# Two-layer trunk on one core: all FFN column blocks by seven products instead of two plain blocks at each start

## The chip, the cores and the metric

The kernel runs on one core of one Trainium2 chip. The metric is the device time of one execution in microseconds (us). TensorE (PE) multiplies matrices; VectorE (DVE) and ScalarE (ACT) work element by element and read PE's results out of PSUM; GpSimd (POOL) does little here; SyncE (SP) issues the loads of weights. Each engine works through its own queue in a fixed order and stands still where an instruction waits for another engine or a transfer.

## The reference

640 tokens (128 context and 512 latent) of width 1024 pass two layers. Each layer is an FFN with half a step, a token mixer, and a second FFN; so there are four FFNs, and they hold most of the work:

```python
def swiglu(h, w_in, w_out):
    u, v = jnp.split(h @ w_in, 2, axis=-1)
    return (jax.nn.silu(u) * v) @ w_out

def ffn_branch(x, mods, g_pre, g_post, w_in, w_out):
    shift, scale, gate = mods
    y = swiglu(modulate(x, g_pre, shift, scale), w_in, w_out)
    return x + FFN_RES * gate * rmsnorm(y, g_post)
```

`w_in` is 1024 x 5632 (u and v of 2816 columns each), `w_out` 2816 x 1024. The mixer of the first layer is a gated delta rule beside a latent attention, that of the second a gated linear attention. All of it is float32.

## The kernel before

**Precision.** A float32 operand is split into a high part (a cast to the fast format, on ACT) and a low part (the difference, on DVE). One product of operands is then high x high, high x low and low x high. `pair` does this for weights (L603 and L604, 128x1024 or 128x512), `parts` for tokens (L513 and L514), `close` for the finished block (L691).

**Blocks and products.** The 22 column blocks t of an FFN take 128 columns of u and 128 of v. Tokens are halved (320 each) and so are the features (four chunks of 128 each), so h is a 2x2 of quarters "11", "21", "12", "22". What this document calls a product is one quarter, or a sum of quarters, times one weight half: 4 chunks x 3 split terms = 12 matmuls of 320 columns (`dot`, L650). Directly, u and v of a block need eight products (96 matmuls). In the other form, `rest` with `begin` and `begun`, seven products (84 matmuls) do it, in the manner of Strassen: 1 and 2 use the quarters "11" and "21" as they are, 6, 5, 7 and 4 use sums of quarters (`t2`, `t1`, `t3`, `t4`), 3 uses "22" after the sums. The sums of tokens are formed once in an FFN (`sums`: four differences, L519, then their splits), the sums of weights in each block (`weights_b`, L620 to L623, then three `pair`s for products 6 and 3, 5, and 7 and 4).

**Order of an FFN before.** Two blocks (`PLAIN`) go by eight products: `plain(t, 0)` for t = 0 and 1 uses the first token half, `plain(t, 1)` the second. Between them blocks 2 to 4 are begun by products 1 and 2 (`early`), which need no sums. Then come `open_c`, the sums, the raw loads and `weights_b` of block 2, and the main loop from t = 2 to 21 with `rest`. From block 5 on, product 1 of the next block is put into `rest` of the one before. From t = 2, too, the `down` products of the two blocks closed before (L298, 512 columns, groups of six matmuls) are put between the products of `rest`, at the places that `SLOTS` names; DVE adds each group to y (L304). While the tokens of the first half come in, the kernel also runs mixer or norm rows; the token quarters are split as they arrive.

**Reading results.** DVE reads the accumulator Y after product 6 (L707: u2), again after product 7 (L715: d1, L717 adds Z) and after product 4 (L724, L725); Z, with products 5 and 3, is read in L717, L742 and L744.

**Buffers.** `rawp` is a ring of seven raw weight buffers of 512 KB, `hlp` has 16 split weight buffers, `Tp` 18 token-wide tiles, `ps_up` three accumulators. A program sets the order within each queue when the kernel is built.

## Time and profile before

| | |
|---|---|
| median of three runs | 2714.4 us (2713.94 to 2716.94) |
| the profiled execution | 2716.26 us |
| its span | 2714.5 us |
| mean granted TensorE clock | 0.991 |
| busy share PE / DVE / ACT / POOL | 97% / 72% / 43% / 5% |
| FFN starts, about | 44, 1015, 1478 and 2269 us |

The span is the time from the first to the last instruction of the profile. Busy times of an engine overlap those of others; matmuls are pipelined, so how long a matmul holds PE is read from the distance between starts and not from the duration of one. The granted clock is the mean TensorE clock in a stretch as a share of full speed. An entry in square brackets behind an instruction is the idle time of its engine just before it and what ended it.

### The profile page before, as it was taken

The numbers are of one execution on the slowest core, as the hardware profiler recorded it, in microseconds if no ns is written. First come the engines' busy times: TensorE is split into PE (matmuls) and PEld (weight loads), VectorE is DVE, ScalarE is ACT, GpSimd is POOL, SyncE is SP. The second block draws the span as 40 slices with busy tenths as digits, with TensorE's granted clock in tenths as the row PEclk, the third lists the DMA queues.
The fourth block names the chain that finished last, engine by engine and source line by source line (L and its number), as shares of the span: only waits on it lengthen the run. The fifth ranks groups of instructions, "written<-read, shape, count | busy, mean of one in ns | idle before, by whom it ended". The sixth has DMA issues, their size and how long they took to land. (4 is left out here: it accounts for less than half of the span.)

```text
span 2714.5 us, 41232 instructions
## 1 busy us (share of the span) xinstructions
PE 2632.5 (97%) x16040; PEld 2331.2 (86%) x16040; DVE 1943.0 (72%) x3731; ACT 1179.1 (43%) x2281; POOL 125.5 (5%) x301
## 2 busy tenths in 40 slices
PE   6999999999999999999999999999999999999998
PEld 4988888789858678888997999999899988999997
DVE  5777777768585558777778777777675749777776
ACT  5433333554345645332335433334765447333333
POOL 0000000200100010000001000000200002000001
PEclk8999999999999999999999999999999999999999
DMA  8334424734151334343227322224212143332222
GB/s 272 123 115 141 148 96 133 251 103 142 50 188 46 128 117 130 114 138 103 86 71 244 104 87 86 86 81 135 92 55 67 59 140 109 95 92 86 78 70 101
DMA packets 297099, 309.60 MB, mean 114 GB/s; under 512 B 13573, under 2 KB 250639, under 8 KB 296903
## 3 DMA queue, kind: packets, MB, share of 16 engines
q1 hardware_dynamic: 278240, 260.05, 30.1%
q10 hardware_dynamic: 18663, 46.92, 4.9%
q8 instruction: 126, 2.06, 0.3%
q14 instruction: 70, 0.57, 0.1%
HBM read 286.59 MB, written 20.33 MB: 113 GB/s over the span
## 5 line engine op out<-in xcount | busy, mean ns | idle before, releaser
L650 PE MATMUL up<-ar,hi 128*128 128x320 f32 x2944 | 658.6, 311 | 10.5 <-ACT ar L513 4.5
L650 PEld LDWEIGHTS up<-ar,hi 128*128 128x128 f32 x2944 | 502.4, 189 | 37.2 <-ACT ar L513 6.1
L650 PE MATMUL up<-ar,lo 128*128 128x320 f32 x1472 | 455.5, 310 | 0.6 <-DVE lo L604 0.6
L603 ACT CAST hi<-raw 128x1024 fp32r<-128x1024 f32 x256 | 268.1, 1050 | 295.4 <-PE up L650 258.4
L304 DVE TENSOR_TENSOR y<-y,dn 128x512 f32<-128x512 f32 x388 | 264.5, 682 | 151.9 <-PE dn L298 150.8
L604 DVE TENSOR_TENSOR lo<-raw,hi 128x1024 fp32r<-128x1024 f32 x256 | 312.4, 1222 | 75.1 <-ACT hi L603 74.5
L298 PE MATMUL dn<-hi,al 128*128 128x512 f32 x880 | 347.8, 395 | 0.1
L298 PE MATMUL dn<-lo,ah 128*128 128x512 f32 x880 | 347.6, 395 | 0.0
L298 PE MATMUL dn<-hi,ah 128*128 128x512 f32 x880 | 346.8, 395 | 0.7 <-DVE y L304 0.5
L650 PE MATMUL up<-hq,hi 128*128 128x320 f32 x1408 | 315.1, 310 | 0.3 <-DVE xn L707 0.3
L650 PEld LDWEIGHTS up<-ar,lo 128*128 128x128 f32 x1472 | 277.9, 189 | 1.3 <-DVE lo L604 1.3
L208 PE MATMUL up<-ar,hi 128*128 128x384 f32 (+1 forms) x1184 | 267.3, 315 | 4.9 <-ACT ar L274 4.0
L650 PEld LDWEIGHTS up<-hq,hi 128*128 128x128 f32 x1408 | 238.8, 188 | 21.5 <-issue 9.2
L650 PE MATMUL up<-hq,lo 128*128 128x320 f32 x704 | 217.4, 309 | 0.0
L208 PEld LDWEIGHTS up<-ar,hi 128*128 128x128 f32 x1184 | 200.6, 191 | 15.3 <-issue 5.6
L183 DVE TENSOR_TENSOR lo<-raw,hi 128x1024 fp32r<-128x1024 f32 x145 | 175.8, 1218 | 45.0 <-ACT hi L182 38.2
L298 PEld LDWEIGHTS dn<-hi,al 128*128 128x128 f32 x880 | 165.3, 188 | 39.3 <-DVE al L691 1.2
L298 PEld LDWEIGHTS dn<-hi,ah 128*128 128x128 f32 x880 | 165.2, 188 | 26.3 <-DVE y L304 1.4
L208 PE MATMUL up<-ar,lo 128*128 128x384 f32 (+1 forms) x592 | 184.3, 311 | 0.0
L298 PEld LDWEIGHTS dn<-lo,ah 128*128 128x128 f32 x880 | 165.1, 188 | 22.2
L182 ACT CAST hi<-raw 128x1024 fp32r<-128x1024 f32 x145 | 150.9, 1048 | 44.5 <-PE up L208 19.0
L658 ACT COPY h<-up 128x320 f32<-128x320 f32 x68 | 29.0, 426 | 314.3 <-PE up L650 314.3
(704 smaller groups left out, 4216.2 us busy)
## 6 DMA issues: line engine op xcount, KB each, us to landing
raw<-in_ffn_w_in_dram SPq DMA_DIRECT2D x188, 512.0 KB
mw<-in_mod_w_dram SPq DMA_DIRECT2D x144, 512.0 KB
raw<-in_ffn_w_out_dram SPq DMA_DIRECT2D x88, 512.0 KB
xdr<-x ACTq DMA_DIRECT2D x25, 512.0 KB
x<-xdr ACTq DMA_DIRECT2D x25, 512.0 KB
raw<-in_od_w_in_dram SPq DMA_DIRECT2D x24, 512.0 KB
raw<-in_ev_w_in_dram SPq DMA_DIRECT2D x19, 512.0 KB
gb<-gate ACTq DMA_DIRECT2D x12, 512.0 KB
```

Of the source, the lines that this page charges most:

```text
L182: nc.scalar.copy(hi, raw)
L183: nc.vector.tensor_sub(lo, raw, hi.bitcast(F32))
L208: self.nc.tensor.matmul(ps[:, :n], lhsT=wt[a][:, kc], rhs=self.h[g][:, b, kc], start=k == 0, stop=k == 3 * KC - 1)
L298: nc.tensor.matmul(ps, lhsT=a(i, m), rhs=w[j][:, nh * 512:nh * 512 + 512], start=k == 0, stop=k == last)
L304: nc.vector.tensor_add(yd, yd, ps)
L603: nc.scalar.copy(hi, raw[:, :n])
L604: nc.vector.tensor_sub(lo, raw[:, :n], hi.bitcast(F32))
L650: nc.tensor.matmul(ps[:, :HT], lhsT=w[i][:, kc], rhs=b[j].at(kc), start=first and n == 0, stop=n == 11, skip_group_check=not first)
L658: self.T.nc.scalar.copy(p1, X[:, :HT])
```

## The change

`PLAIN` and `plain` go. `EARLY` is 7 instead of 5: the first seven blocks begin with products 1 and 2, and the main loop runs from t = 0 instead of 2. Down products still start at t = 2. The quarter "12" is no longer split, and its four tiles go; `Tp` is 20 instead of 18 and `rawp` 6 instead of 7. The prefetch loads u of three blocks where it was u and v of two. For the first seven blocks u is loaded twice, once for products 1 and 2 and once for `weights_b`.

```diff
@@ -27,9 +27,8 @@
 GROUPS = ((0, 384), (384, 256))
 HW = (6400, 4096)
 HT = TOK // 2
-PLAIN = 2
 FILLS = (((16, 6), (10, 6)), ((18, 0), (0, 0)))
-EARLY = 5
+EARLY = 7
 SLOTS = ((2, 3, 4, 5, 6), (0, 1, 2, 3, 4))
 TW = 648
 MFILL = ((1, 1, 1, 1, 1, 1, 0), (1, 1, 1, 1, 1, 1, 0), (1, 0, 1, 0, 1, 0, 0), (0, 0, 0, 0, 0, 0, 0))
@@ -87,9 +86,9 @@
         self.cst = mk("cst", 1)
         self.hp = mk("hp", 1)
         self.xp = mk("xp", 5)
-        self.rawp = mk("rawp", 7)
+        self.rawp = mk("rawp", 6)
         self.hlp = mk("hlp", 16)
-        self.Tp = mk("Tp", 18)
+        self.Tp = mk("Tp", 20)
         self.sml = mk("sml", 2)
         self.ps_up = mk("ps_up", 3, space=PSUM)
         self.ps_dn = mk("ps_dn", 2, space=PSUM)
@@ -490,11 +489,8 @@
         return [Quad((t, 4 * HT * (j + i), 0, 4)) for i in range(2)]
 
     def open_b(self):
-        T = self.T
-        self.a1 = T.arena(1)
-        t = [T.T(F32R, "hq") for _ in range(4)]
+        self.a1 = self.T.arena(1)
         self.B["22"] = self.pair_in(self.a1, 0)
-        self.B["12"] = [Quad((t[2 * j], 0, 0, 2), (t[2 * j + 1], 0, 2, 2)) for j in range(2)]
 
     def open_c(self):
         T = self.T
@@ -554,8 +550,7 @@
         if span:
             if m == 3:
                 self.open_b()
-            for n in ("12", "22"):
-                self.parts(self.F[n], n, *span)
+            self.parts(self.F["22"], "22", *span)
             self.spans.append(span)
 
     def first(self, mods, rows):
@@ -580,7 +575,8 @@
                     for o, e, s in segs:
                         t = xT[half * 4 + j][:, o:e]
                         T.modulate(t, t, s, half * 4 + j, *self.mod, j % 2)
-                    self.parts(self.F[n], n, 0, HT, (j,))
+                    if n in self.B:
+                        self.parts(self.F[n], n, 0, HT, (j,))
         self.spans.append((0, HT))
 
 
@@ -628,12 +624,10 @@
     def weights_d(self, t):
         self.wd[t] = self.T.prep_rows(self.w_out, t * P)
 
-    def prefetch(self, ts=range(PLAIN)):
+    def prefetch(self, ts=range(3)):
         for t in ts:
             if (t, 1) not in self.w:
                 self.weights_a(t)
-            if (t, "v1") not in self.w:
-                self.pair(t, self.load(DFF + t * P), "v1", "v2")
 
 
 
@@ -662,24 +656,6 @@
         self.product(X, t, 2, False, True)
         self.T.nc.scalar.activation(s1, X[:, :HT], AF.Silu)
         self.began[t] = None, p1, s1
-
-    def plain(self, t, g):
-
-        T, nc = self.T, self.T.nc
-        if g == 0:
-            self.began[t] = T.T(name="o")
-        o = self.began[t]
-        oc = o[:, g * HT:(g + 1) * HT]
-        for names, v in (((1, 2), False), (("v1", "v2"), True)):
-            ps = T.up()
-            for j, name in enumerate(names):
-                self.dot(ps, self.w[t, name], f"{j + 1}{g + 1}", j == 0, j == 1)
-            if v:
-                nc.vector.tensor_mul(oc, oc, ps[:, :HT])
-            else:
-                nc.scalar.activation(oc, ps[:, :HT], AF.Silu)
-        if g == 1:
-            self.close(t, self.began.pop(t)[:, :TOK])
 
     def close(self, t, a, c=0):
 
@@ -766,22 +742,16 @@
     def run(self, nxt):
         T, n, e, sts = self.T, NFT, EARLY, {}
         self.todo, self.slots = None, ()
-        for t in range(PLAIN):
-            self.plain(t, 0)
-        for t in range(PLAIN, e):
-            self.weights_a(t)
+        for t in range(e):
+            self.prefetch((t,))
             self.early(t)
-        for t in range(PLAIN):
-            self.plain(t, 1)
         self.open_c()
         for c, w in self.spans:
             self.sums(c, w)
         st = T.S([P, D], "xn", 1)
-        self.raws(PLAIN)
-        self.weights_b(PLAIN)
-        for t in range(PLAIN):
-            self.weights_d(t)
-        for t in range(PLAIN, n):
+        self.raws(0)
+        self.weights_b(0)
+        for t in range(n):
             if t + 1 < n:
                 self.raws(t + 1)
             if e <= t + 1 < n:
@@ -799,7 +769,7 @@
             if t % 2 == 1 and t < n - 4:
                 self.weights_d(t - 1)
                 self.weights_d(t)
-            if self.fills[0] > t - PLAIN:
+            if self.fills[0] > t - 2 >= 0:
                 self.filler()
             if self.later and t == 5:
                 self.later()
```

As counts of the whole program: PE has 14,794 matmuls after 14,890; DVE 3,736 instructions after 3,670 (eight more 1024-wide and eight more 512-wide low halves of weights, eight more of each of L620 to L623 and of the evacuations in `rest`, 16 fewer of L678 and some 40 fewer token splits); SP 525 after 509 (16 more loads of 512 KB).

The order of PE at the second FFN start, before: the last rows of the second plain block (v of the second token half, into `up1318`), and then product 6 of block 2 into `up1346`. `ar` and `hq` are token splits, `hi`, `lo` and `hilo` weight splits.

```order
L650 MATMUL up1318_9867<-ar1284_9531,hi1249_9370 128x320 x2
L650 MATMUL up1318_9867<-ar1284_9531,lo1250_9371 128x320
L650 MATMUL up1346_9990<-hq1321_9897,hi1333_9963 128x320 [waits DVE_49]
L650 MATMUL up1346_9990<-hq1322_9898,hi1333_9963 128x320
L650 MATMUL up1346_9990<-hq1321_9897,lo1334_9964 128x320
```

After: the last rows of block 6's product 2 into `up1316`, then product 6 of block 0 into `up1336` and its product 5 into `up1337`.

```order
L644 MATMUL up1316_9754<-ar1238_9267,hi1313_9749 128x320 x2
L644 MATMUL up1316_9754<-ar1238_9267,lo1314_9750 128x320
L644 MATMUL up1336_9862<-hq1317_9781,hi1329_9847 128x320 [waits Activation_49]
L644 MATMUL up1336_9862<-hq1318_9782,hi1329_9847 128x320 [waits DVE_49]
L644 MATMUL up1337_9876<-hq1319_9783,hilo1331_9851 128x320 [waits Activation_49]
L644 MATMUL up1337_9876<-hq1321_9785,hilo1331_9851 128x320 [waits DVE_49]
L644 MATMUL up1336_9862<-hq1317_9781,lo1330_9848 128x320 [waits DVE_49]
```

The plain products that stood ahead of the first sums product are gone; products of early blocks stand there, 168 matmuls in place of 264. Further on in block 0, PE's order after is product 7, product 4 and product 3 with nothing in between:

```order
L644 MATMUL up1336_9862<-hq1324_9788,lo1333_9855 128x320
L644 MATMUL up1336_9862<-ar1238_9267,hi1332_9854 128x320 [waits DVE_49]
...
L644 MATMUL up1336_9862<-ar1238_9267,lo1333_9855 128x320
L644 MATMUL up1337_9876<-ar1287_9531,hi1329_9847 128x320 [waits DVE_49]
```

The first of these rows is the last of product 7, the second begins product 4, the last begins product 3. In blocks from 2 on, rows of down products (L298 before, L288 after) stand between them.

The order of DVE at the same start, before: behind the last token split, the low halves of block 2's weights, the down weights' splits (L183), an evacuation and the closing of a plain block (L678, L691), and the weight sums of block 3.

```order
L514 TENSOR_TENSOR hq1328_9904<-f1231_9260,hq1328_9904 128x128 [waits Activation_49]
L604 TENSOR_TENSOR lo1334_9964<-raw1330_9954,hi1333_9963 128x1024 [waits PE_49,Activation_49]
L604 TENSOR_TENSOR hilo1335_9967<-s11332_9958,hilo1335_9967 128x512 [waits DMAHW5_49,Activation_49]
L604 TENSOR_TENSOR lo1337_9971<-raw1331_9956,hi1336_9970 128x1024 [waits PE_49,Activation_49]
L183 TENSOR_TENSOR lo1340_9977<-raw1338_9974,hi1339_9976 128x1024 [waits DMAHW2_49,DVE_49,Activation_49]
L678 TENSOR_TENSOR o1292_9577<-o1292_9577,up1314_9811 128x320 [waits PE_49]
L183 TENSOR_TENSOR lo1343_9983<-raw1341_9980,hi1342_9982 128x1024 [waits DMAHW4_49,Activation_49]
L691 TENSOR_TENSOR al1316_9838<-o1292_9577,ah1315_9837 128x640 [waits Activation_49]
L620 TENSOR_TENSOR s11361_10110<-raw1345_9988 128x512 [waits DMAHW7_49]
```

After: behind the last token split, the low halves of block 0's weights, the evacuation of block 0's product 6 (L683), and weight sums and low halves of block 1 (L616 to L619, L600) between the evacuations of block 0.

```order
L510 TENSOR_TENSOR ar1287_9531<-f1236_9265,ar1238_9267 128x128 [waits Activation_49]
L600 TENSOR_TENSOR lo1330_9848<-raw1326_9838,hi1329_9847 128x1024 [waits PE_49]
L600 TENSOR_TENSOR hilo1331_9851<-s11328_9842,hilo1331_9851 128x512 [waits DMAHW0_49,Activation_49]
L600 TENSOR_TENSOR lo1333_9855<-raw1327_9840,hi1332_9854 128x1024 [waits PE_49,Activation_49]
L683 TENSOR_TENSOR xn1325_9837<-up1336_9862,e1291_9561 128x320 [waits PE_49]
L616 TENSOR_TENSOR s11340_9936<-raw1335_9860 128x512 [waits DMAHW1_49,DVE_49]
L617 TENSOR_TENSOR raw1335_9860<-raw1334_9858,raw1335_9860 128x512 [waits DMAHW7_49,DVE_49]
L618 TENSOR_TENSOR raw1334_9858<-s11340_9936,raw1334_9858 128x512 [waits DVE_49]
L600 TENSOR_TENSOR hilo1343_9945<-s11340_9936,hilo1343_9945 128x512 [waits Activation_49]
L619 TENSOR_TENSOR raw1334_9858<-raw1334_9858 128x512 [waits DVE_49]
L691 TENSOR_TENSOR xn1325_9837<-up1336_9862,e1291_9561 128x320 [waits PE_49]
```

The evacuations of `rest` (L683, L691 after) now stand where the plain block's last evacuation and the down weights' splits stood.

## Rows read from the trace of the kernel before

**Rows 1.** The page's first part: busy us, share of the span, instructions, by engine

```profile
PE 2632.5 (97%) x16040; PEld 2331.2 (86%) x16040; DVE 1943.0 (72%) x3731; ACT 1179.1 (43%) x2281; POOL 125.5 (5%) x301
```

**Rows 2.** Windows of three main loops: stretch, us, busy per engine, PEclk, DMA share, GB/s

```profile
88.00:460.00 372.00, 367.85 (x2201) 329.66 (x2200) 266.37 (x404) 123.36 (x169) 0.00 (x0) 1.00 0.39 124
1064.00:1424.00 360.00, 359.94 (x2146) 328.05 (x2145) 267.18 (x400) 124.07 (x173) 0.00 (x0) 1.00 0.33 103
2324.00:2660.00 336.00, 336.00 (x1989) 312.53 (x1988) 251.03 (x377) 117.88 (x163) 0.00 (x0) 1.00 0.25 77
```

**Rows 3.** Windows of the four stretches ahead of the first sums product: PE, PEld, DVE, ACT, POOL

```profile
45.00:82.00 37.00, 35.98 (x221) 34.96 (x221) 36.61 (x76) 30.39 (x63) 0.00 (x0) 0.91 0.35 110
1014.00:1062.00 48.00, 43.47 (x278) 41.43 (x278) 45.09 (x87) 33.11 (x75) 6.36 (x9) 0.96 0.46 141
1484.00:1517.00 33.00, 33.00 (x223) 31.92 (x222) 32.36 (x65) 20.97 (x47) 0.00 (x0) 1.00 0.46 144
2285.00:2314.00 29.00, 29.00 (x196) 28.40 (x195) 28.70 (x61) 18.31 (x42) 0.00 (x0) 1.00 0.32 96
```

**Rows 4.** Timeline of PE in a steady block: start, us, engine, line, operation

```profile
107.19 1.92 PE L650 MATMUL up<-hq,hilo 128*128 128x320 f32 x12
108.95 0.39 PE L298 MATMUL dn<-hi,ah 128*128 128x512 f32 x1
...
111.27 0.40 PE L298 MATMUL dn<-lo,ah 128*128 128x512 f32 x1
```

**Rows 5.** Timeline of DVE ahead of the first sums product, at the four starts

```profile
68.80 4.64 DVE L514 TENSOR_TENSOR hq<-xT,hq 128x320 fp32r<-128x320 f32 x11
...
80.00 2.35 DVE L604 TENSOR_TENSOR lo<-raw,hi 128x1024 fp32r<-128x1024 f32 x2
...
1049.45 3.51 DVE L514 TENSOR_TENSOR hq<-f,hq 128x576 fp32r<-128x576 f32 x9 [0.27 <-ACT hq L513]
...
1053.05 1.23 DVE L604 TENSOR_TENSOR lo<-raw,hi 128x1024 fp32r<-128x1024 f32 x1
1054.20 0.68 DVE L604 TENSOR_TENSOR hilo<-s,hilo 128x512 fp32r<-128x512 f32 x1
1054.84 1.23 DVE L604 TENSOR_TENSOR lo<-raw,hi 128x1024 fp32r<-128x1024 f32 x1
...
1058.65 0.81 DVE L691 TENSOR_TENSOR al<-o,ah 128x640 fp32r<-128x640 f32 x1
1059.38 0.68 DVE L620 TENSOR_TENSOR s<-raw 128x512 f32<-128x512 f32 x1
...
1061.55 0.70 DVE L623 TENSOR_TENSOR raw<-raw 128x512 f32<-128x512 f32 x1
...
1507.97 1.21 DVE L604 TENSOR_TENSOR lo<-raw,hi 128x1024 fp32r<-128x1024 f32 x1
...
2305.11 1.22 DVE L604 TENSOR_TENSOR lo<-raw,hi 128x1024 fp32r<-128x1024 f32 x1 [0.20 <-ACT hi L603]
```

**Rows 6.** Timeline of PE: the first matmuls of the first sums product, four starts

```profile
88.31 0.46 PE L650 MATMUL up<-hq,hi 128*128 128x320 f32 x2
...
1063.13 0.46 PE L650 MATMUL up<-hq,hi 128*128 128x320 f32 x2
...
1519.03 0.46 PE L650 MATMUL up<-hq,hi 128*128 128x320 f32 x2
...
2314.03 0.46 PE L650 MATMUL up<-hq,hi 128*128 128x320 f32 x2
```

**Rows 7.** A wait of PE (timeline), and PE-only windows around it: PE busy, PEclk

```profile
998.47 1.90 PE L257 MATMUL pt<-ident,xn 128*128 128x128 f32 x8 [2.78 <-DVE xn L252]
...
995.00:1000.00 5.00, 2.22 (x12) 0.85 0.26 105
1000.00:1005.00 5.00, 5.00 (x22) 0.81 0.00 0
1005.00:1010.00 5.00, 5.00 (x30) 1.00 0.00 0
```

## The prediction

> **What bounds the kernel now.** I read the busy shares first. TensorE (PE) computes in 97% of the span and VectorE (DVE) in 72% [rows 1], so taking matmuls away should shorten the kernel by their length, wherever DVE can follow. Whether it can is a matter of the stretch, so I read the busy time of the engines stretch by stretch. In three main loops PE is busy for 367.85 of 372, 359.94 of 360 and 336.00 of 336 us, and DVE for only 266, 267 and 251 of these [rows 2]: there PE alone sets the pace. In the stretches just before the first product on token sums, it is different: PE 35.98 and DVE 36.61 of 37 us, 43.47 and 45.09 of 48, 33.00 and 32.36 of 33, 29.00 and 28.70 of 29 [rows 3]. Both engines are full there. DVE splits weights and tokens and forms the sums in these stretches, and PE works off products that need no sums. The 96% and 72% of the whole span are means over two different kinds of stretch, and the change removes matmuls in the second kind only.
>
> **What it removes: 96 matmuls.** Twelve matmuls of one product went from 107.19 to 108.95, so 1.76 us, or 0.1467 us each [rows 4]. An FFN has two blocks that now take 84 instead of 96 matmuls: 24 x 0.1467 = 3.52 us for each FFN, 14.1 us for four. That is the whole possible gain, if PE never waits for it.
>
> **What it moves: the first sums product comes 96 matmuls earlier.** Before, 264 matmuls stand ahead of it (two plain blocks of 96, three early ones of 24); after, seven early blocks of 24, so 168. PE so gets there 96 x 0.1467 = 14.1 us earlier. (That this equals the total saving is chance: here it is 96 matmuls in one FFN.) What PE needs there comes from DVE: the sums, their splits and then the low halves of the first weights. How long before PE's arrival was that ready? The low half of products 6 and 3 was begun at 80.00, 1053.05, 1507.97 and 2305.11 [rows 5]; one such operation takes 1.15 us of DVE's time (1053.05 to 1054.20), so it ended at 81.15, 1054.2, 1509.1 and 2306.25. PE's first sums product began at 88.31, 1063.13, 1519.03 and 2314.03 [rows 6]. The slack is 7.2, 8.9, 9.9 and 7.8 us, 33.8 together.
>
> **How much earlier can DVE be?** Since it is full in these stretches [rows 3], only by what is taken from its queue ahead of that point: the four splits of the operand "12", eleven such 320-wide operations took 4.64 us [rows 5], 0.42 each, and two products of plain blocks (L678) of the same width: 6 x 0.42, 2.5 us; I take 2.4, since at the later starts "12" is cut into other pieces. The order of DVE's queue does not put the weights of block 0 ahead of the sums' splits in exchange; at the third and fourth start four or five of its 512-wide weight sums even come behind them, at 0.72 us each (1059.38 to 1061.55 for three) [rows 5], which I leave out of the first sum and use as a bound. So PE waits 14.1 - 2.4 = 11.7 us less the slack: 4.5, 2.8, 1.8 and 3.9 us, **13.0 us** together. Going through the queues row by row, with the later weight sums counted, I got 3.4, 4.4, 2.8 and 5.2, 15.8 together; the two differ by 2.8 us, and I keep the smaller one.
>
> **What it adds: two blocks that DVE sets.** Blocks 0 and 1 ran their products without any sums; now they are `rest` blocks, but no down product runs beside them, since there is no closed pair yet. One costs PE 60 matmuls (products 6, 5, 7, 4, 3), 8.8 us. DVE needs for one: four 512-wide sums at 0.72 = 2.9, two 1024-wide low halves at 1.15 = 2.3, one 512-wide low half at 0.64 (1054.20 to 1054.84), seven 320-wide evacuations at about 0.42 = 2.9 and the split of the closed block at 0.73 (1058.65 to 1059.38) [rows 5]: 9.5 us. In the same stretch come the two splits of down weights, 2.3 us. Two blocks so take 21.3 us of DVE and 17.6 of PE: up to 3.7 us a start if none of it is done ahead, nothing if the block-1 weights were prepared while PE waited. In steady blocks there is cover: seven products and 30 down matmuls at 0.23 us (108.95 to 111.27 for ten) [rows 4] are 19 us of PE, and DVE is busy for 72 to 75% of it [rows 2]; this cover is what is missing in blocks 0 and 1. Two waits inside a block can be named. Product 4 stands directly behind product 7 on the accumulator that DVE's addition of product 7 (L715 before, L691 after) has to read first; before, a down group stood between. And PE's product 7 accumulates into what DVE's addition of product 6 reads. I take **2 us a start, 8 in all**, between 0 and 3.7, nearer to the middle since the queue is a strict order and the block-1 sums come between block-0 evacuations. Later than block 1, nothing new: blocks 2 to 6 carry downs and have 24 matmuls fewer than a steady block (8.8 + 7.0 = 15.8 us of PE, against some 14 of DVE), and DVE catches up.
>
> **The clock.** PE waited for 2.78 us up to 998.47; in 995 to 1000, which holds that wait, the granted clock was 0.85, in the next 5 us 0.81, and then 1.00 [rows 7]. That is 0.75 + 0.95 = 1.7 us lost behind one such wait. Each start now gets a wait of this size where there was none. Most of this falls in blocks 0 and 1, where DVE and not PE is late, so I take **0.5 us a start, 2 in all**, between 0 and 1.7 each.
> A rule speaks of the same: the Trainium skill, page "TensorE: Matmul & The Clock Gate", Part 1: The HAM clock gate, says that "the default state is throttled, and activity releases the throttle." By it each of the four waits would end with PE at 1.2 GHz instead of 2.4, and the sum would be 4 x 1.7 - 2 = 4.8 us longer. The trace agrees that a wait of 2.8 us is followed by a lower clock [rows 7], but whether waits of 1.8 us are, no row here shows.
>
> **Loads.** Blocks 0 to 6 now load u twice (early and as raws): 16 loads of 512 KB more, and the ring of raw buffers is six instead of seven. The transfers are 0.25 to 0.39 of the DMA engines' time in the main loops and 0.32 to 0.46 in the starts [rows 2, 3], so bandwidth covers them; 0 us. If one of block 1's raws comes late by a buffer, DVE's queue holds behind its first weight sum, and all evacuations of block 0 with it: that is the third rival.
>
> **Sum.** -14.1 (matmuls) + 13.0 (waits at the first sums product) + 8 (blocks 0 and 1) + 2 (clock) = +8.9, say +9 us on the profiled execution of 2716.26 us. It ran 1.86 us above the median 2714.4, so the forecast on the median is **2723.5 us**. I checked this by what counts at the end: how much later block 2's product 5 ends, taking the order of both queues row by row. I got 8.0, 8.1, 8.2 and 10.7 us later; from there on PE has 48 matmuls fewer (7.0 us), so +1.0, +1.1, +1.2 and +3.7, which is +7. Bounds: with first waits alone, -14.1 + 13.0 = -1; if a third of these waits is hidden too, -6; with all upper ends, 15.8 + 14.8 + 6.8 - 14.1 = +23.
>
> **Rivals.**
> Wash, 2713 us (2709 to 2720): only the first waits come, blocks 0 and 1 cost nothing since DVE goes on with their weights while PE waits. For it: the waits give DVE 13 us of lead. Against it: DVE is full, so this is no lead but its own lateness, and the block sum of 9.5 against 8.8 us leaves nothing to catch up with.
> Faster, 2705 us (2700 to 2709): DVE is paced by PE there more than the busy shares tell, so that it comes earlier as PE does. A low half can be written only when the products that used its buffer are done, and PE now does those earlier. It decides when DVE gains 5 us a start instead of 2.4 and stays ahead in blocks 0 and 1: then the first waits fall from 13.0 to some 3, blocks 0 and 1 cost 2 in all, and -14.1 + 3 + 2 = -9, which is 2705; the limit is -14.1, 2700. For it: at the second start DVE idles for 2.9 of 48 us [rows 3], and 0.27 us ahead of nine splits at 1049.45 [rows 5]. Against it: at the other three starts it idles for 0.3 to 0.6 us.
> Much slower, 2740 us (2735 to 2745): the clock falls after each wait and after the smaller ones in blocks 0 and 1 (4 x 1.7 + 4 x 1.7), and the raws of block 1 come late from a ring of six: +20 to +30. Against it: the share of DMA.
> That the change doesn't remove the matmuls can be excluded: the order of PE's queue shows 14,794 matmuls for 14,890.
>
> **How the numbers follow.** Chances: forecast (2720 to 2735) 0.52, wash 0.27, faster 0.13, much slower 0.08. The range 2709 to 2735 leaves out the faster case and the much slower one, 0.21. A measurement of this kernel can tell about 0.2%, 5.4 us, from no change: faster is under 2709, slower over 2719.8. So faster 0.13, same 0.27, slower 0.60.
>
> **What would show it.** Right: at each of the four starts a PE wait of 2 to 5 us ahead of the first `up<-hq,hi` matmul, released by DVE; in blocks 0 and 1 more PE waits of 0.3 to 1.5 us released by `xn` or `e` evacuations; DVE at 95% or more over the 25 us around them; the granted clock under 1.0 in one or two 5 us windows behind; PE's busy time 14 us less, in the main loops from block 3 on no change. Wrong: DVE reaches the first low half more than 5 us earlier than before, counted from the FFN's start, or blocks 0 and 1 run at 9 us each with no wait: then the kernel is at 2709 or faster. Waits of DVE on loads in blocks 0 and 1 would speak for the much slower case.

## The result

The changed kernel is slower: 2752.05 us median (2748.42 to 2753.29) against 2715.59 us for the kernel before in the same comparison, a ratio of 1.0132 with a 95% interval of 1.0115 to 1.0150. That is +36 us where +9 was forecast; the direction was right, the size was not, and the time lies outside the range of 2709 to 2735.

The page's first part of the changed kernel (busy us, share, instructions), to be read beside [rows 1]:

```profile
PE 2645.8 (96%) x15944; PEld 2328.8 (85%) x15944; DVE 1987.8 (72%) x3797; ACT 1186.3 (43%) x2283; POOL 124.9 (5%) x301
```

96 matmuls fewer, as the order showed; yet PE is busy for 13 us more and the span is 2750.1 instead of 2714.5 us. The granted clock of the span is 0.986 instead of 0.991; over 2750 us that is some 14 us. To see where the time goes, I cut both spans at PE's first and last product of each run of FFN work:

| stretch | before, us | after, us | difference |
|---|---|---|---|
| start to the end of the first FFN | 481.2 | 491.6 | +10.4 |
| even mixer, to the first product of the second FFN | 534.4 | 546.0 | +11.6 |
| second and third FFN | 876.8 | 880.1 | +3.3 |
| odd mixer, to the first product of the fourth FFN | 376.6 | 384.5 | +7.9 |
| fourth FFN, to the end | 445.4 | 447.8 | +2.4 |

The mixers have no block of an FFN in them; yet 11.6 us are lost in the first of them and 7.9 in the second. The prediction had nothing for either stretch.

At the third and the fourth FFN start the profile shows what was forecast, a PE wait of 2 to 5 us ahead of the first `up<-hq,hi` matmul. At the first start the wait is 0.79 us, and at the second there is none ahead of that matmul but waits of 0.74 and 1.62 us just behind it. PE's timeline at the third and the fourth start (start, us, engine, line, operation, idle time before and its releaser), which answers to [rows 6]:

```profile
1532.38 0.90 PE L644 MATMUL up<-hq,hi 128*128 128x320 f32 x2 [4.41 <-ACT hi L599]
...
2329.72 0.56 PE L644 MATMUL up<-ar,hi 128*128 128x320 f32 x2 [0.52 <-ACT e L652]
...
2337.09 0.90 PE L644 MATMUL up<-hq,hi 128*128 128x320 f32 x2 [5.35 <-ACT hi L599]
```

DVE's timeline over that last wait, which answers to [rows 5]:

```profile
2331.39 2.10 DVE L510 TENSOR_TENSOR hq<-f,hq 128x384 fp32r<-128x384 f32 x6
2333.40 0.76 DVE L510 TENSOR_TENSOR ar<-f,ar 128x384 fp32r<-128x384 f32 x2
2334.07 0.69 DVE L618 TENSOR_TENSOR raw<-s,raw 128x512 f32<-128x512 f32 x1
2334.67 0.69 DVE L600 TENSOR_TENSOR hilo<-s,hilo 128x512 fp32r<-128x512 f32 x1
2335.27 0.69 DVE L619 TENSOR_TENSOR raw<-raw 128x512 f32<-128x512 f32 x1
2335.88 0.69 DVE L616 TENSOR_TENSOR s<-raw 128x512 f32<-128x512 f32 x1
2336.60 0.69 DVE L617 TENSOR_TENSOR raw<-raw,raw 128x512 f32<-128x512 f32 x1
2337.21 1.22 DVE L600 TENSOR_TENSOR lo<-raw,hi 128x1024 fp32r<-128x1024 f32 x1
```

The wait names ACT's cast, but that cast takes the weight sums, and they (L618, L619) stand behind the token splits in a DVE queue without a gap. So DVE sets this moment, at 2337, and PE stands for 5.35 us.

The granted clock behind these two waits (windows: stretch, us, busy per engine, then PEclk, DMA share and GB/s):

```profile
1532.00:1538.00 6.00, 5.62 (x28) 5.54 (x29) 5.35 (x7) 3.06 (x4) 0.00 (x0) 0.72 0.48 154
...
2336.00:2342.00 6.00, 4.91 (x20) 4.82 (x21) 5.31 (x7) 3.06 (x4) 0.00 (x0) 0.56 0.38 117
```

### The profile page after: what moved, and what is told of

The parts are those of the page before. It is cut to its first block, busy times and chain, and to the rows that moved or that the text cites. A ratio compares the mean times of both kernels' runs of the same rounds, so it can differ in the third digit from the quotient of the medians.

```text
span 2750.1 us, 41117 instructions
## 1 busy us (share of the span) xinstructions
PE 2645.8 (96%) x15944; PEld 2328.8 (85%) x15944; DVE 1987.8 (72%) x3797; ACT 1186.3 (43%) x2283; POOL 124.9 (5%) x301
## 5 line engine op out<-in xcount | busy, mean ns | idle before, releaser
L644 PE MATMUL up<-ar,hi 128*128 128x320 f32 x2816 | 630.1, 311 | 13.7 <-ACT e L652 5.7
L644 PEld LDWEIGHTS up<-ar,hi 128*128 128x128 f32 x2816 | 479.3, 189 | 43.0 <-ACT e L652 8.7
L644 PE MATMUL up<-ar,lo 128*128 128x320 f32 x1408 | 435.1, 310 | 0.8 <-DVE lo L600 0.6
L599 ACT CAST hi<-raw 128x1024 fp32r<-128x1024 f32 x264 | 276.0, 1051 | 318.2 <-PE up L644 223.7
L600 DVE TENSOR_TENSOR lo<-raw,hi 128x1024 fp32r<-128x1024 f32 x264 | 322.1, 1222 | 59.9 <-ACT hi L599 59.0
L644 PEld LDWEIGHTS up<-ar,lo 128*128 128x128 f32 x1408 | 265.2, 189 | 2.5 <-DVE lo L600 1.6
L207 PEld LDWEIGHTS up<-ar,hi 128*128 128x128 f32 x1184 | 201.6, 192 | 17.0 <-issue 7.1
L182 DVE TENSOR_TENSOR lo<-raw,hi 128x1024 fp32r<-128x1024 f32 x145 | 176.2, 1220 | 52.0 <-ACT hi L181 42.7
L181 ACT CAST hi<-raw 128x1024 fp32r<-128x1024 f32 x145 | 150.8, 1049 | 68.3 <-PE up L207 23.0
L644 PE MATMUL up<-hq,hilo 128*128 128x320 f32 x1056 | 172.8, 313 | 0.7 <-ACT hilo L599 0.7
```

What stands on the lines that cost most here:

```text
L181: nc.scalar.copy(hi, raw)
L182: nc.vector.tensor_sub(lo, raw, hi.bitcast(F32))
L207: self.nc.tensor.matmul(ps[:, :n], lhsT=wt[a][:, kc], rhs=self.h[g][:, b, kc], start=k == 0, stop=k == 3 * KC - 1)
L599: nc.scalar.copy(hi, raw[:, :n])
L600: nc.vector.tensor_sub(lo, raw[:, :n], hi.bitcast(F32))
L644: nc.tensor.matmul(ps[:, :HT], lhsT=w[i][:, kc], rhs=b[j].at(kc), start=first and n == 0, stop=n == 11, skip_group_check=not first)
```

## What the other stretches pointed to

A diff line that I had priced at 0 us is the one that reaches into the mixers: the ring of raw weight buffers is six instead of seven. Of the modulation weights (`mw`, 144 loads of 512 KB), 128 go through the same ring; the other 16, of the first 2,048 columns, use another pool. `adaln`, the routine of the modulation, holds up to four buffers until it has multiplied two chunks, and an FFN block holds two. Idle time of PE and of its weight loads just before the modulation matmuls (us, times), in the kernel before:

```profile
  DMA mw<-in_mod_w_dram: 12.7, 9
```

and in the changed kernel:

```profile
  DMA mw<-in_mod_w_dram: 25.9, 31
```

SyncE's queue in the even mixer (waits: instruction, what released it, us in total, times, longest us), before:

```profile
SPq L376 <- PE ad L395: 96.8, 14, 29.0
SPq L196 <- PE ad L395: 9.5, 5, 3.9
```

and after:

```profile
SPq L195 <- PE ad L394: 56.9, 9, 34.9
SPq L375 <- PE ad L394: 54.5, 13, 29.3
```

L196 (L195 after) issues the mixer's own weight loads, L376 (L375) those of the modulation weights. The mixer's loads now wait for 57 us in the place of 10 for a modulation matmul to give a buffer free. Both kinds of load together wait hardly longer for it than before (111 and 106 us); what has changed is which load stands in the queue. This is an observation on queues; whether the ring is the cause was for runs to settle. **Theory A:** the ring costs the larger part, the FFN starts about 9 us as forecast. **Theory B:** the converted blocks cost all of it.

## The ring taken by itself

Three kernels: the old one with six buffers, the changed one with seven (which needs one token-wide tile less), and the changed one with that tile less alone.

```diff
-        self.rawp = mk("rawp", 7)
+        self.rawp = mk("rawp", 6)
```

> The kernel before with a ring of six raw weight buffers instead of seven, nothing else. Theory A (the ring is what I had at 0 us): the loads of mixer weights, of the modulation weights and of the FFN go through this ring, so it is slower by 18 to 26 us, 2734 to 2742, most of it in the two mixers (+12 and +8) and in the middle of the first FFN (+8), with the FFN starts unchanged. Theory B (the two converted blocks cost all of the 36 us): within 3 us of the kernel before.

Measured: 2735.39 us, ratio 1.0080 (1.0065 to 1.0095), +20 us.

```diff
-        self.rawp = mk("rawp", 6)
+        self.rawp = mk("rawp", 7)
-        self.Tp = mk("Tp", 20)
+        self.Tp = mk("Tp", 19)
```

> The changed kernel with seven raw buffers; to make room, token-wide tiles are 19 instead of 20. Theory A: it loses only at the FFN starts, 2720 to 2730. Theory B: 2748 to 2755 as the changed kernel.

Measured: 2724.37 us, ratio 1.0038 (1.0023 to 1.0053), +9.1 us.

> The changed kernel with 19 token-wide tiles and its six raw buffers: what the tile given up in the run with seven raw buffers costs by itself. Theory A and B: 2748 to 2756, within 4 us of the changed kernel. If it is over 2760, the run with seven buffers can't be read as the ring alone.

Measured: 2748.56 us, ratio 1.0127 (1.0110 to 1.0144), as the changed kernel, and the order of PE's queue is the same in both. So the tile is worth nothing, and the seventh buffer 24 us.

Theory B falls. Cut as above, against the kernel before (spans of single profiled executions, so a microsecond or two is not to be read):

| stretch | changed | changed, seven buffers | before, six buffers |
|---|---|---|---|
| to the end of the first FFN | +10.4 | -1.9 | +6.3 |
| even mixer | +11.6 | -1.7 | +12.4 |
| second and third FFN | +3.3 | +2.0 | -2.6 |
| odd mixer, to the first product of the fourth FFN | +7.9 | +6.1 | -0.6 |
| fourth FFN | +2.4 | +2.2 | +0.3 |

The ring costs in the first FFN and the even mixer, where the modulation weights are worked off. My expectation of +8 us in the odd mixer from the ring was a miss: the old kernel with six buffers loses nothing there, and the changed one with seven still has most of it. So the conversion, not the ring, goes with the loss in the odd mixer, though no block of an FFN runs there.

Most of it comes at the very end of that stretch, 4.5 of the 6.1 us in its last 10 us, just ahead of the fourth FFN's first product. PE's timeline and windows there, before:

```profile
2261.82 0.50 PE L298 MATMUL dn<-hi,ar 128*128 128x512 f32 x1 [2.00 <-DVE y L304]
2264.44 1.06 PE L257 MATMUL pt<-ident,xn 128*128 128x128 f32 x8 [0.48 <-DVE xn L252]
...
2264.00:2269.00 5.00, 4.56 (x24) 3.94 (x25) 4.19 (x9) 2.98 (x7) 1.08 (x3) 1.00 0.01 3
```

and in the changed kernel with seven buffers, with a line of DVE between them (a window's row gives the stretch, its us, the busy us of PE, PEld, DVE, ACT and POOL, then the granted clock, the DMA share and GB/s):

```profile
2262.91 0.50 PE L297 MATMUL dn<-hi,ar 128*128 128x512 f32 x1 [3.02 <-DVE y L303]
2266.11 1.94 PE L256 MATMUL pt<-ident,xn 128*128 128x128 f32 x8 [1.50 <-DVE xn L251]
...
2260.40 1.22 DVE L600 TENSOR_TENSOR lo<-raw,hi 128x1024 fp32r<-128x1024 f32 x1
...
2264.00:2269.00 5.00, 3.50 (x14) 2.86 (x13) 3.71 (x7) 2.19 (x7) 2.70 (x6) 0.54 0.18 55
```

PE waits for DVE 2.0 us longer, and the granted clock is 0.54 where it was 1.00. In DVE's queue a weight split of the fourth FFN stands at 2260.40, ahead of the additions that PE waits for. That this split is the cause is read from the queue and was not tested by a run.

## Which occupants of the ring

Is six too few because modulation weights sit in it (A1), or for the FFN's and the mixers' own loads alone (A2)? The first try let `adaln` multiply chunk by chunk, holding two buffers instead of four:

```diff
-   for k, wt, j in [(k, wt, j) for k, wt in held for j in range(nj)] if one or kc % 2 else []:
+   for k, wt, j in [(k, wt, j) for k, wt in held for j in range(nj)]:
...
-   if one or kc % 2:
-       held = []
+   held = []
```

> The kernel before with six raw buffers, in which the modulation weights are multiplied chunk by chunk: two buffers are held at a time instead of four. Theory A1 (four held for modulation and two for the next FFN block fill a ring of six, so the next load cannot start): the +6 us in the middle of the first FFN and the first +3 of the even mixer go, what is left is the late load of the latent weights, 2719 to 2726. Theory A2 (the ring is too short for the loads of FFN and mixer by themselves): it stays at 2731 to 2740.

Measured: 2728.19 us, ratio 1.0054 (1.0039 to 1.0069): 7 us less than with six buffers, 14 above the kernel before, between the two expectations.

> The same chunk-by-chunk modulation with seven raw buffers as before: what that edit costs or gives by itself. Both theories: within 4 us of the kernel before, 2711 to 2719.

Measured: 2715.81 us, 1.0003 (0.9994 to 1.0013), no change. With six buffers the first FFN lost nothing any more (-3.8 us to its end), but the even mixer was 11.4 us longer than before, against 3.2 us with seven buffers and the same edit.

The second try went for the one load on which PE visibly waited in the even mixer with six buffers (waits of PE):

```profile
PE up L1488 <- DMA ukv<-in_ev_mla_w_ukv_dram: 3.9, 1, 3.9
```

SyncE's timeline of the old kernel with six buffers showed it right behind nine modulation loads (start, us, engine, line, operation):

```profile
751.59 24.13 SPq L376 DMA_DIRECT2D mw<-in_mod_w_dram  x9
775.82 0.37 SPq L1479 DMA_DIRECT2D ukv<-in_ev_mla_w_ukv_dram  x1
```

With seven buffers it stands there too, but goes out 6 us ahead of its matmul, and PE has no wait for it:

```profile
739.89 22.49 SPq L376 DMA_DIRECT2D mw<-in_mod_w_dram  x9
762.95 0.33 SPq L1479 DMA_DIRECT2D ukv<-in_ev_mla_w_ukv_dram  x1
```

The edit moves this load to ACT's queue:

```diff
-        nc.sync.dma_start(ukv, i["ev_mla_w_ukv"][0])
+        nc.scalar.dma_start(ukv, i["ev_mla_w_ukv"][0])
```

> The kernel before with six raw buffers, the load of the latent up-projection (ukv) issued from ScalarE's queue instead of SyncE's. With six buffers SyncE issued it at 775.8, behind nine loads of modulation weights that waited for raw buffers, and TensorE waited 3.9 us for it. Theory A3 (what the ring holds back is everything queued behind on SyncE, not only what uses the ring): 4 to 8 us less than with six buffers, 2727 to 2732. If ukv is late for another reason (the DMA engines are full), no gain, 2733 to 2740.

Measured: 2734.87 us, 1.0078 (1.0064 to 1.0092): no gain. Issued from ACT's queue it went out at 773.70, and PE waited 4.1 us. So theory A3 (what stands behind on SyncE) falls for this load; why it goes out so late there as well, I did not find.

> The changed kernel, six raw buffers, with both remedies: modulation weights held by two and ukv on ScalarE's queue. If the loss by the ring is the same in the changed kernel as in the one before, 10 to 16 us less than 2750, so 2734 to 2740; the rest to 2724 would be the mixer's own loads.

Measured: 2750.91 us, 1.0135 (1.0120 to 1.0151): a miss, no gain in the changed kernel. Its first FFN ended 12 us earlier than in the changed kernel, and its even mixer, second and third FFN took 13 us longer: what was not waited for early was waited for later.

The third try takes the modulation weights out of the ring altogether. Behind the first 2,048 columns their loads are left out, and the matmuls run on one fixed tile of 512 columns:

```diff
-   w = self.W(name="mw") if (l, q) == (0, 0) else self.raw("mw")
+   if (l, q) != (0, 0):
+       wt.append(self.mwc)
+       continue
+   w = self.W(name="mw")
...
+   self.mwc = self.cst.tile([P, 512], F32, name="mwc")
+   nc.sync.dma_start(self.mwc, mod_w[0, 0:P, 0:512])
...
```

> The kernel before, seven raw buffers, without the loads of the modulation weights behind the first 2,048 columns: their matmuls run on one fixed tile of 512 columns, and nothing of them passes the ring. It is the reference for the next two. Both theories: 2700 to 2714, since waits for these loads (some 13 us of idle time around the modulation matmuls) go.

Measured: 2702.00 us, 0.9958 (0.9944 to 0.9971).

> The same with six raw buffers. Theory A1 (the modulation weights in the ring are what makes six too few): within 5 us of the run with seven. Theory A2 (six are too few for the FFN's and the mixers' own loads): 14 to 22 us above it.

Measured: 2701.60 us, 0.9957 (0.9943 to 0.9971). Whether there are six buffers or seven makes no difference any more.

> The changed kernel with its six raw buffers and without the loads of the modulation weights, as above. Theory A1: 8 to 13 us above the kernel before with seven buffers and without these loads, as the changed kernel is with seven buffers (+9). Theory A2: 28 to 38 us above it.

Measured: 2708.60 us, 0.9983 (0.9974 to 0.9992): 6.6 us above the kernel before under the same conditions, a little under the expected 8 to 13.

That decides against A2: the ring of six costs 20 to 24 us only while the modulation weights pass through it. It doesn't show by itself what in their passing costs, since the edit takes away 128 transfers of 512 KB together with their place in the ring. A run that keeps the loads in buffers of their own was not made.

In the first FFN the waits show the way. Idle time of PE and of its weight loads there, just before modulation matmuls (us, times): none of it is for `mw` with seven buffers, before or after the change. With six it is, in the old kernel

```profile
  DMA mw<-in_mod_w_dram: 8.4, 9
```

and in the changed one

```profile
  DMA mw<-in_mod_w_dram: 8.2, 12
```

So PE waits for modulation weights that came too late. How the even mixer turns the smaller ring into time is only partly seen. Named idle time of PE there rose by only 2.6 us (15.8 to 18.4) of 12. Windows over the same work, from the first matmul of L1232 to the first of L1488, in the kernel before:

```profile
685.80:769.10 83.30, 81.21 (x671) 68.62 (x668) 53.27 (x166) 33.36 (x87) 11.13 (x14) 0.98 0.28 98
```

and with six buffers:

```profile
696.20:784.40 88.20, 83.88 (x665) 70.06 (x661) 53.97 (x170) 33.34 (x87) 11.99 (x14) 0.94 0.30 97
```

Nearly the same matmuls took 4.9 us more, 2.7 of it with PE busy, and the granted clock was 0.94 instead of 0.98. At 6% and 2% of the stretch that is 5.3 against 1.7 us lost to the clock: 3.6 us. Two other stretches of the mixer show 0.96 and 0.94 in the place of 1.00. So waits too short or too scattered to head a list may come back through the clock; that is read from the windows and was not tested by a run. Against it stands that over the whole execution the granted clock is 0.991 with six buffers as with seven. A rival was not tested either: with one buffer less the build sets another order of the queues. 1,493 of the 16,040 rows of PE's queue then stand elsewhere, 1,210 of them in the even mixer; for the pair without modulation loads it is 313, 51 of them in the even mixer. Part of the 12 us may so come from the order and not from waiting for a buffer.

## The converted blocks by themselves

With seven buffers the change costs +9.1 us, the size that was forecast for the whole (how far for the forecast's reasons, stands further down). PE's timeline at its third and fourth start:

```profile
1506.50 0.81 PE L644 MATMUL up<-hq,hi 128*128 128x320 f32 x2 [2.95 <-ACT hi L599]
...
2300.48 0.56 PE L644 MATMUL up<-ar,hi 128*128 128x320 f32 x2 [0.68 <-ACT e L652]
...
2306.69 0.90 PE L644 MATMUL up<-hq,hi 128*128 128x320 f32 x2 [4.18 <-ACT hi L599]
```

and the windows at the first, second, third and fourth start:

```profile
76.00:86.00 10.00, 8.84 (x58) 8.07 (x57) 9.59 (x13) 4.83 (x6) 0.00 (x0) 1.00 0.37 108
1050.00:1060.00 10.00, 8.98 (x61) 8.72 (x61) 9.97 (x18) 3.82 (x5) 0.00 (x0) 1.00 0.52 146
1506.00:1512.00 6.00, 5.50 (x26) 5.31 (x27) 5.33 (x7) 3.07 (x4) 0.00 (x0) 0.72 0.42 128
2306.00:2312.00 6.00, 5.31 (x20) 5.23 (x21) 5.54 (x8) 2.34 (x3) 0.00 (x0) 0.50 0.39 121
```

DVE is full in the first two. The third is the first 6 us of block 0 behind a wait of 2.95 us, the fourth behind 4.18 us, at half the clock.

**Is it DVE?** The rival (D) takes the name in the brackets at its word: ACT's casts. Run without DVE's weight sums of blocks 0 and 1:

```diff
-        nc.vector.tensor_add(s1, v1, v2)
+        if t >= 2:
+            nc.vector.tensor_add(s1, v1, v2)
...
-        self.pair(t, s1, 5)
+        self.pair(t, s1 if t >= 2 else v1, 5)
```

> The changed kernel with seven raw buffers (2724.4), without the four weight sums of blocks 0 and 1 of each FFN; the products run on the unsummed weights. It leaves out eight VectorE operations of 0.72 us, 5.8 us a start. Theory C (VectorE sets the time of the first sums product and of blocks 0 and 1): 12 to 20 us less, 2704 to 2712. Theory D (the casts on ScalarE, which the waits name, set it): within 4 us of 2724.

Measured: 2712.53 us, 0.9997 (0.9988 to 1.0006): 11.8 us less than with the sums, just short of the 12 to 20 that C (DVE sets it) expected and far from D. At the fourth start the wait of 4.18 us is gone; two of 0.74 and 1.61 us are left inside block 0:

```profile
2297.86 0.56 PE L645 MATMUL up<-hq,hilo 128*128 128x320 f32 x2 [0.74 <-ACT hilo L599]
2300.03 0.64 PE L645 MATMUL up<-hq,lo 128*128 128x320 f32 x1 [1.61 <-DVE lo L600]
```

Even so it is no faster than the kernel before: the 14.1 us of matmuls were not had even without these sums.

**Can GpSimd take the sums?** It is idle at three of the four starts and busy for 6.36 of 48 us at the second [rows 3].

```diff
+        e = nc.gpsimd if t < 2 else nc.vector
-        nc.vector.tensor_add(s1, v1, v2)
+        e.tensor_add(s1, v1, v2)
```

(and the three differences likewise)

> The changed kernel with seven raw buffers (2724.4), the four weight sums of blocks 0 and 1 on GpSimd instead of VectorE. Theory C: 8 to 18 us less, 2706 to 2716, if one such sum takes GpSimd under 1.5 us and does not slow VectorE. If GpSimd takes 3 us or more for one, or VectorE's operations get longer beside it, 2725 to 2740.

Measured: 2760.18 us, 1.0173 (1.0157 to 1.0188): worse by 36 us, a miss, slower than even the bad case allowed. One sum took (lines of GpSimd, whose spans are rough: count, busy us, mean ns)

```profile
L617 POOL TENSOR_TENSOR s<-raw 128x512 f32<-128x512 f32 x8 | 14.2, 1776 | 116.8 <-DVE hilo L600 88.8 <-DMA raw<-in_ffn_w_in_dram 28.0
```

1.78 us against 0.72 us in DVE's chain [rows 5]. Four in a row and twice an FFN do not make 36 us by themselves; the rest was not followed up.

**How far ahead may PE come?** Fewer early blocks bring PE to the first sums product sooner still: the changed kernel with five early blocks, seven raw buffers and 18 token-wide tiles.

> The changed kernel with five instead of seven early blocks, seven raw buffers, 18 token-wide tiles. 48 matmuls fewer stand ahead of the first sums product of each start, 7.0 us. If DVE sets the time of that product, as I hold, PE waits 7 us more at each start, less what the first two blocks then need not wait: +20 to +28 against the run with seven early blocks and seven buffers, about 2742 to 2755. If PE's own work sets it (the rival by which DVE comes earlier with PE), within 5 us of that run.

Measured: 2741.38 us, 1.0103 (1.0088 to 1.0118): 17 us more than with seven early blocks, under the 20 to 28 expected but of the sign and near the size that a DVE-set moment demands, and far from the rival's 5. (One tile less than in the kernel it is compared with is in this edit too, and was not run alone.)

**One plain block instead of two** keeps half of the saving and a larger lead of products.

```diff
-PLAIN = 2
+PLAIN = 1
...
-        for t in range(PLAIN):
-            self.weights_d(t)
...
-            if self.fills[0] > t - PLAIN:
+            if self.fills[0] > t - 2 >= 0:
```

Besides the plain block, the edit drops the early splits of down weights, which now come behind block 1 in the main loop, and lets the rows that fill in (`filler`) begin at block 2 as before.

> One plain block instead of two, blocks 1 to 4 early, seven raw buffers, 18 token-wide tiles. Half of the matmul saving, 48 in the whole, 7.0 us; 192 instead of 264 matmuls stand ahead of the first sums product, so TensorE comes 10.6 us earlier against slacks of 7.2, 8.9, 9.9 and 7.8: waits of 3.4, 1.7, 0.7 and 2.8, 8.6 together, and one block without down products, 1 to 2 us a start. Theory C: 2714.4 - 7.0 + 8.6 + 4 to 8 = 2720 to 2725.

Measured: 2722.43 us, 1.0032 (1.0021 to 1.0044), as expected.

> The same with blocks 1 to 5 early: 216 matmuls ahead, TensorE 7.0 us earlier, less than each of the four slacks. Theory C: no wait at the first sums product, only the one block without down products, 1 to 2 us a start: 2714.4 - 7.0 + 4 to 8 = 2711 to 2716, faster than the run with one early block less by 6 to 10. If the saved matmuls never count because VectorE sets these stretches altogether, 2716 to 2722.

Measured: 2720.69 us, 1.0024 (1.0014 to 1.0035). A miss for theory C in its simple form (2711 to 2716): at three of the four starts PE has no wait at the first sums product, and the time is still above the expectation, only 1.7 us below the run before. It lies in the range given for the other case, that DVE sets these stretches altogether and the saved matmuls never count (2716 to 2722). In its trace PE waited early in the first FFN for a weight that the kernel before has split ahead:

```profile
59.24 0.56 PE L650 MATMUL up<-ar,hi 128*128 128x320 f32 x2 [4.28 <-ACT hi L603]
```

> One plain block, blocks 1 to 5 early, as in the run of 2720.7, with the weights of blocks 1 and 2 also loaded and split ahead of the FFN, as the kernel before does for its first two blocks. The trace of that run has a wait of 4.3 us at 59 for the split of such a weight. If that is the loss: 2712 to 2718. If VectorE has only got more to do at the same place: 2719 to 2723.

Measured: 2721.49 us, 1.0031 (1.0020 to 1.0042), no gain, as its second case had it (2719 to 2723): that wait shrank,

```profile
59.65 0.55 PE L653 MATMUL up<-ar,hi 128*128 128x320 f32 x2 [1.53 <-ACT o L683]
```

and the first FFN ended 4 us earlier, but the odd mixer and the fourth FFN together took 4 us longer. What makes these late was not located. No version that was run with its full work beats the kernel before.

## Why the prediction was right and wrong

**Failed: the loads, "0 us".** The step looked at the DMA engines' busy share (0.25 to 0.46) and concluded that bandwidth covers a ring of six. The ring is a count of buffers, and the question is who holds them and for how long. I named the FFN's raws as its users and left out the modulation and mixer weights, though they are on the same page of the profile: 128 of the 144 modulation loads and 59 loads of the mixers, of the same size. The rows that would have told are the waits of SyncE's queue for a buffer and the 12.7 us idle ahead of modulation matmuls, nine times already with seven buffers. Measured: +20.1 us in the kernel before, +24.2 in the changed one, 0 without the modulation weights. In the first FFN PE waits 8.4 us for modulation weights with six buffers and never with seven; how the even mixer loses its 12 us stays open in part.

The third rival did say that "the raws of block 1 come late from a ring of six". In the changed kernel DVE has one wait for a raw at the second start, 1.35 us, and it is for block 0. Its price, 2735 to 2745, is the nearest to the result, and still 7 us short. The result came near that price for another reason; the rival's other half, a lower clock, did come (0.986 for 0.991 over the span).

**The FFN starts.** First sums product: 13.0 us of waits were forecast (4.5, 2.8, 1.8, 3.9). With seven buffers the waits there and on the last early blocks' accumulators (L652) are 1.5, 3.1, 3.5 and 4.9 us, 12.9 together before rounding. That the sums agree to 0.1 us is partly luck: the single starts are off by up to 3 us, 2.6 us of the 12.9 are waits for ACT's reading of early accumulators, which the forecast didn't have, and 2.4 us at the second start lie inside block 0. The mechanism, that PE comes first and waits for DVE, is borne out at the third and fourth start and by the run without the sums.

**Blocks 0 and 1 and the clock.** From the first sums product to the end of block 1's product 3, the four starts took 19.8, 22.9, 20.5 and 22.1 us. First rows of block 2 stand among them, so that they hold 128, 122, 128 and 130 matmuls, 74.5 us of PE's own time. Less the 2.4 us of the second start already counted, 8.4 us were lost, where 8 + 2 were forecast. But the parts were not these: the clock took some 4.5 us (1.7 at the third start and 2.8 at the fourth) in the place of 2, and waits 3.9 in the place of 8. The two errors offset each other, which is luck. At the fourth start the granted clock was 0.50 for 6 us: 3 us, nearly twice what [rows 7] gave for one wait and six times the 0.5 that I took for a start.

**The sum.** -14.1 + 12.9 + 8.4 = +7.2; measured +9.1 in the median, +6.7 in the span. The time lies elsewhere than forecast, though. The FFNs come to -1.9, +2.8, +0.5 and +2.2, where I had +1.0, +1.1, +1.2 and +3.7, between the second and the third it is -1.3, the even mixer has -1.7, and the odd mixer +6.1, for which there was no term. So that the size of the converted blocks came out is in part luck, too. The page of the changed kernel with seven buffers begins:

```profile
PE 2626.1 (97%) x15944; PEld 2320.7 (85%) x15944; DVE 1986.4 (73%) x3797; ACT 1185.4 (44%) x2283; POOL 126.8 (5%) x301
```

PE's busy time fell by 6 us and not by the forecast 14, with a granted clock of 0.989 instead of 0.991 (5 to 7 us), and its idle time rose by 13. Differences of 2 us between such sums can't be read from single executions. Two slips hang on nothing: PE's share is given once as 96% where the page has 97%, and the sum on the median is 2723.3 by its own terms.

**The low clock behind each wait.** After waits of 2.95 and 4.18 us the granted clock was 0.72 and 0.50 over 6 us, which is 1.7 and 3.0 us. After waits of 0.74 and 1.62 us at the second start it was 1.00 in the kernel with seven buffers and 0.66 in the changed kernel, behind the same two waits (the first row is of the kernel with seven, the second of the changed one):

```profile
1046.00:1051.00 5.00, 4.22 (x29) 4.22 (x30) 4.84 (x7) 0.62 (x1) 0.00 (x0) 1.00 0.47 143
...
1074.00:1079.00 5.00, 4.76 (x22) 4.76 (x23) 4.08 (x7) 0.00 (x0) 0.00 (x0) 0.66 0.67 192
```

The Trainium skill, page "TensorE: Matmul & The Clock Gate", Part 1: The HAM clock gate, says that the throttled state is the default and that activity releases it. The trace agrees with it behind the two long waits, and behind the short ones in one run of two. What the prediction worked out from it, that each of the four waits ends at the low clock (6.8 us), is not what the runs show: in the kernel with seven buffers the clock cost some 4.5 us in blocks 0 and 1 of the third and fourth start, and at the first two starts it stayed at 1.00 in the windows above.

**Rivals.** Faster fell: DVE came no earlier with PE (the run with five early blocks). The wash fell: blocks 0 and 1 did cost, 8.4 us.

## What to carry to other kernels

A smaller pool is a change of its own, and its price is not read from bandwidth: list every tile that is taken from it, in all phases of the program, see who waits for a release already (the queue of the loads shows it), and expect the loss in stretches that the diff does not mention. Matmuls saved at a place where VectorE is as busy as TensorE turn into waiting, and into clock behind the waiting; compare the arrival of both engines at the first product that needs both. When a result is four times the forecast in the right direction, test the smallest line of the diff by itself first. And when a part comes out at its forecast size, look whether the time is lost where the forecast put it: here 6.1 of 6.7 us lay in a stretch that had no term.

## What was not expected of the hardware

A 128x512 sum took 1.78 us on GpSimd where the four of a chain took 0.72 us each on VectorE, and the three differences behind it 1.30 to 1.43 us. The granted clock after a wait of 4.18 us was 0.50 over 6 us, the lower of the two levels (1.2 and 2.4 GHz) for all of it, and 0.72 after 2.95 us. The same two short waits, 0.74 and 1.62 us, were followed by 1.00 in one kernel and by 0.66 in another.
